# Two transfers cut smaller: the third x load in halves, and the last stores in finer pieces

## The chip, the cores and the metric

The kernel runs on one core of one Trainium2 chip. The metric is the device time of one execution in microseconds (us), as a median of repeated runs. All runs quoted here were with a granted TensorE clock of 0.95 to 1.00. A profile of one execution comes with each kernel. Its span (209.1 us before) is about 2 us shorter than the device time (211.0 us).

## The reference

```python
# x [16, 512, 1024], weight [1024, 768], bias [768], residual [16, 512, 768], all float32
return (np.matmul(x, weight) + bias + residual).astype(np.float32)
```

The kernel has to read 61.9 MB and write 25.2 MB. The matmul runs in bf16.

## The kernel before

There are 8192 rows: 64 tiles of 128 rows, in 8 super tiles of J = 8 tiles. A tile's x is cast to bf16 on ScalarE and transposed on TensorE. It then meets the weights in 8 steps of two matmuls each, 512 and 256 columns wide. GpSimd and VectorE add bias and residual into the residual's own buffer `ro`, and the result is stored from there. All large transfers are issued by one queue, that of SyncE (SP), in program order.

```python
J = 8; X_BUFS = 2; RO_BUFS = 4            # x: 2 super tiles in SBUF, residual/result: 4

def load_x(S, j0=0, j1=J):                # tiles j0..j1 of super tile S
    if S < n_s:
        if j0 == 0:
            x_sb[S] = ring(sb, "x_tile", S, X_BUFS, [P, J, K], FP32)
        K_(nc.sync.dma_start(out=x_sb[S][:, j0:j1, :], in_=x_d[S, :, j0:j1, :]))

def store(S, j0=0, j1=J, n0=0, nl=N):
    K_(nc.sync.dma_start(
        out=out_d[S, :, j0:j1, n0:n0 + nl], in_=ro[S][:, j0:j1, n0:n0 + nl]))
# ... (head: loads, weight casts, the first HEAD = 3 tiles)
for t in range(HEAD, n_t):
    cast(t + 2)
    S, j = divmod(t, J)
    if (t + 2) % J == J - 1:
        load_x(S + X_BUFS)
        load_res(S + X_BUFS)
        if 1 <= S < n_s - 1:
            store(S - 1)
    # ... (matmuls of tile t, transposes of t + 1, adds)
    if S == n_s - 1 and j == 0:
        store(S - 1)
    if S == n_s - 1 and j == J // 2:
        store(S, 0, J // 2)
    if S == n_s - 1 and j == J - 1:
        store(S, J // 2, j)               # tiles 4, 5 and 6 of the last super tile
t, S = n_t - 1, n_s - 1
for b, (n0, nl) in enumerate(chunks):     # last tile: 512 columns, then 256
    # ... (matmuls, add)
    store(S, J - 1, J, n0, nl)
```

## Time and profile before

| | before |
|---|---|
| device time, median of 6 runs | 211.01 us (210.88 to 211.19) |
| TensorE busy, share of the span | 96% |
| transfers of the SP queue, packet time as a share of 16 DMA engines' span | 97.8% |
| TensorE's one late wait for data | at 56 us, 0.8 to 0.9 us |
| last store: issued, landed | 204.9, 208.2 us |

These are lines of the page of the kernel before. "DMA" and "GB/s" cut the span into 40 slices. A digit is the busy share in tenths, as a mean over the core's 16 DMA engines. The `q` lines are DMA queues: packets, MB, and their packets' time as a share of 16 engines' span.

```profile
span 209.1 us, 3149 instructions
PE 201.1 (96%) x1274; PEld 130.8 (63%) x1299; DVE 105.0 (50%) x139; ACT 68.0 (33%) x68; POOL 115.6 (55%) x71
...
DMA  6999999999999999999999999999999999999966
GB/s 229 428 422 432 430 421 438 443 456 407 404 476 420 409 432 412 443 428 434 437 415 459 415 414 447 437 426 418 428 431 443 445 412 421 432 442 423 414 287 273
...
q1 hardware_dynamic: 5328, 87.03, 97.8%
q8 instruction: 10, 0.16, 0.3%
...
PE 70%; DMA 25%; issue 1%; ACT 1%; DVE 0%; POOL 0%; ACTq 0%; POOLq 0%
```

TensorE and the DMA engines are both full. The last line is the chain of waits that ended last. It is a quarter DMA, because it passes through loads of the head and of x. The longest piece of it is the third x load, of which these are the lines (start, duration, what):

```profile
22.74 33.22 DMA x_tile<-in_x_dram
...
56.05 1.05 ACT xb L87
...
57.15 0.66 PE pt L95 x4
```

The timeline of TensorE there (start, duration, engine, line, operation) shows how much this costs. L95 are a tile's transposes, 3.04 us apart in the steady state. Here one gap is 3.86 us.

```profile
53.29 0.60 PE L95 MATMUL pt<-ident,xb 128*128 128x128 f32 x4
...
57.15 0.66 PE L95 MATMUL pt<-ident,xb 128*128 128x128 f32 x4 [0.67 <-ACT xb L87]
...
60.25 0.60 PE L95 MATMUL pt<-ident,xb 128*128 128x128 f32 x4
```

At the end, these are the last three stores as SP issues them. The first is tiles 4 to 6; the `x2` are the two pieces of tile 7.

```profile
202.93 0.33 SPq L78 DMA_DIRECT2D out_dram<-ro  x1
...
204.39 1.55 SPq L78 DMA_DIRECT2D out_dram<-ro  x2
```

The table of stretches for the end follows (window, length, busy time and count of each engine, clock, DMA share, GB/s). The last two columns are what to read: the DMA share falls to 0.32 and recovers once the last stores are issued.

```profile
200.00:201.00 1.00, 1.00 (x9) 0.74 (x8) 0.43 (x1) 0.00 (x0) 0.00 (x0) 1.00 0.90 381
201.00:202.00 1.00, 1.00 (x8) 0.60 (x7) 0.32 (x2) 0.00 (x0) 0.00 (x0) 1.00 0.67 283
202.00:203.00 1.00, 1.00 (x7) 0.43 (x5) 0.90 (x1) 0.00 (x0) 0.00 (x0) 1.00 0.32 135
203.00:204.00 1.00, 1.00 (x9) 0.71 (x8) 0.33 (x1) 0.00 (x0) 0.00 (x0) 1.00 0.41 172
...
206.00:207.00 1.00, 0.00 (x0) 0.00 (x0) 0.00 (x0) 0.00 (x0) 0.00 (x0) 1.00 0.85 340
207.00:208.00 1.00, 0.00 (x0) 0.00 (x0) 0.00 (x0) 0.00 (x0) 0.00 (x0) 1.00 0.68 238
```

### The profile page before, as it was taken

What the parts mean: (1) busy time and instruction counts of PE and PEld (TensorE: products, weight loads), DVE (VectorE), ACT (ScalarE), POOL (GpSimd) and SP (SyncE); (2) the same over time, 40 slices, a digit from 0 to 9 for tenths busy, and PEclk for the clock granted to TensorE, in tenths of its full rate; (3) what the DMA queues carried; (4) which work ended last, traced back from release to release, by engine and by line L of the source; (5) the groups of instructions that cost most, each with busy time, mean ns of one, the idle gap of its engine ahead of it and who ended that gap; (6) DMA issues with size and microseconds to landing.
All of it is one profiled execution on the core that took longest, in us unless ns stands there. A gap on an engine that the chain in (4) does not pass through costs nothing.

```text
span 209.1 us, 3149 instructions
## 1 busy us (share of the span) xinstructions
PE 201.1 (96%) x1274; PEld 130.8 (63%) x1299; DVE 105.0 (50%) x139; ACT 68.0 (33%) x68; POOL 115.6 (55%) x71
## 2 busy tenths in 40 slices
PE   7999999999899999999999999999999999999991
PEld 2556666666566666666666666666666666666660
DVE  0646564455354455445545544554554455446551
ACT  2544315520283054323423252440543234322000
POOL 2000197819936655999499802994069900799000
PEclk9999999999999999999999999999999999999999
DMA  6999999999999999999999999999999999999966
GB/s 229 428 422 432 430 421 438 443 456 407 404 476 420 409 432 412 443 428 434 437 415 459 415 414 447 437 426 418 428 431 443 445 412 421 432 442 423 414 287 273
DMA packets 5344, 87.23 MB, mean 417 GB/s; under 512 B 593, under 2 KB 721, under 8 KB 1618
## 3 DMA queue, kind: packets, MB, share of 16 engines
q1 hardware_dynamic: 5328, 87.03, 97.8%
q8 instruction: 10, 0.16, 0.3%
q14 instruction: 4, 0.03, 0.0%
q10 hardware_dynamic: 2, 0.00, 0.0%
HBM read 61.87 MB, written 25.17 MB: 416 GB/s over the span
## 4 chain that ended last, share of the span: by engine, by line
PE 70%; DMA 25%; issue 1%; ACT 1%; DVE 0%; POOL 0%; ACTq 0%; POOLq 0%
PE po L104 60%; DMA x_tile<-in_x_dram 23%; PE pt L95 10%; DMA tmp<-in_bias_dram 2%; ACT xb L87 1%; DVE ro L131 0%; POOL ident masks.py:197 0%; ACTq L87 0%; POOL tmp L135 0%; POOLq L262 0%
## 5 line engine op out<-in xcount | busy, mean ns | idle before, releaser
L104 PE MATMUL po<-w_sb,xt 128*128 128x512 bf16 (+1 forms) x999 | 175.4, 324 | 1.4
L104 PEld LDWEIGHTS <-xt 128*128 128x128 bf16 x1024 | 100.1, 98 | 59.5 <-DVE xt L99 0.5
L87 ACT CAST xb<-x_tile 128x1024 bf16<-128x1024 f32 x62 | 63.2, 1045 | 115.5 <-PE pt L95 63.2
L121 POOL TENSOR_TENSOR ro<-ro,bias_sb 128x768 f32<-128x768 f32 x40 | 71.2, 1816 | 34.6 <-DMA ro<-in_residual_dram 24.6
L99 DVE COPY xt<-pt 128x512 f32<-128x512 f32 x64 | 44.2, 692 | 88.3 <-PE pt L95 88.2
L121 POOL TENSOR_TENSOR ro<-ro,tmp 128x768 f32<-128x768 f32 x24 | 43.1, 1816 | 42.3 <-DMA ro<-in_residual_dram 25.0
L131 DVE TENSOR_TENSOR ro<-po,ro 128x768 f32<-128x768 f32 (+2 forms) x41 | 38.0, 930 | 2.9 <-PE po L104 2.8
L95 PE MATMUL pt<-ident,xb 128*128 128x128 f32 x256 | 38.6, 274 | 0.7 <-ACT xb L87 0.7
L95 PEld LDWEIGHTS pt<-ident,xb 128*128 128x128 f32 x256 | 30.1, 142 | 9.2 <-ACT xb L87 1.3
L129 DVE TENSOR_TENSOR tmp<-po,bias_sb 128x768 f32<-128x768 f32 x24 | 22.8, 949 | 0.4 <-PE po L104 0.4
L170 PE MATMUL po<-warm 128*128 128x512 bf16 x15 | 6.1, 579 | 1.2 <-DVE warm L156 1.2
L176 ACT CAST w_sb<-ro 128x768 bf16<-128x768 f32 x4 | 3.3, 832 | 4.0 <-DMA ro<-in_weight_dram 4.0
L170 PEld LDWEIGHTS <-warm 128*128 128x128 bf16 x15 | 1.9, 132 | 4.1 <-issue 2.8
L87 DVE CAST xb<-x_tile 128x1024 bf16<-128x1024 f32 x2 | 1.4, 694 | 5.1 <-DMA x_tile<-in_x_dram 5.1
L178 DVE CAST w_sb<-ro 128x768 bf16<-128x768 f32 x4 | 2.2, 556 | 2.2 <-DMA ro<-in_weight_dram 2.2
L161 ACT ACT_TABLE_LOAD x1 | 1.3, 1283 | 2.0 <-POOL ident masks.py:199 2.0
L190 PE MATMUL po<-tmp 128*128 128x512 f32 (+1 forms) x4 | 1.5, 486 | 0.0
L198 DVE COPY bias_sb<-po 128x768 f32<-128x768 f32 x1 | 1.0, 958 | 0.1
L190 PEld LDWEIGHTS po<-tmp 128*128 128x128 f32 x4 | 0.7, 190 | 0.5 <-issue 0.5
L135 POOL MEMSET tmp<- 128x768 f32 x1 | 0.7, 737 | 0.3 <-POOLq L262 0.3
L156 DVE MEMSET warm<- 128x256 uint32 x1 | 0.3, 272 | 0.9 <-PEq L262 0.9
masks.py:199 POOL TENSOR_SCALAR_AFFINE_SELECT ident<-ident 128x128 f32<-128x128 f32 x1 | 0.3, 292 | 0.1
(8 smaller groups left out, 1.0 us busy)
## 6 DMA issues: line engine op xcount, KB each, us to landing
x_tile<-in_x_dram SPq DMA_DIRECT2D x6, 4096.0 KB, 29.4
ro<-in_residual_dram SPq DMA_DIRECT2D x7, 3072.0 KB, 18.0
out_dram<-ro SPq DMA_DIRECT2D x7, 3072.0 KB, 24.9
x_tile<-in_x_dram SPq DMA_DIRECT2D x2, 2048.0 KB, 23.9
x_tile<-in_x_dram SPq DMA_DIRECT2D x3, 1024.0 KB, 8.7
ro<-in_weight_dram SPq DMA_DIRECT2D x4, 768.0 KB, 9.1
ro<-in_residual_dram SPq DMA_DIRECT2D x2, 1536.0 KB, 20.9
out_dram<-ro SPq DMA_DIRECT2D x1, 1536.0 KB, 10.4
```

What stands on the lines that cost most here:

```text
L87: K_(copy(out=xb[t], in_=x_sb[t // J][:, t % J, :]))
L95: K_(nc.tensor.transpose(out=pt[:, c, :], in_=pairs[:, c * P:(c + 1) * P], identity=ident))
L99: K_(nc.vector.tensor_copy(out=xt[t], in_=pt))
L104: K_(nc.tensor.matmul(po[t][:, n0:n0 + nl], lhsT=both[:, e, :], rhs=w_sb[:, c, e, n0:n0 + nl], start=(i == 0), stop=(i == len(steps) - 1),))
L121: K_(nc.gpsimd.tensor_add(out=r, in0=r, in1=tmp[t] if t < EARLY else bias_sb))
L129: K_(nc.vector.tensor_add(out=tmp[t], in0=p, in1=bias_sb))
L131: K_(nc.vector.tensor_add(out=row(t, n0, nl), in0=p, in1=row(t, n0, nl)))
L161: K_(nc.scalar.copy(out=warm_a, in_=warm_a))
L170: K_(nc.tensor.matmul(warm_ps[:, 0:512], lhsT=warm[:, 0:P], rhs=warm, start=True, stop=True))
L176: K_(nc.scalar.copy(out=w_sb[:, c, e, :], in_=w_st[:, c, e, :]))
L178: K_(nc.vector.tensor_copy(out=w_sb[:, c, e, :], in_=w_st[:, c, e, :]))
L190: K_(nc.tensor.matmul(bias_ps[:, n0:n0 + nl], lhsT=ones, rhs=bias_row[:, n0:n0 + nl], start=True, stop=True,))
```

## The change

The intent is to remove the wait at 56 us, by making the first half of x available as soon as it has landed, and to shorten the end, by sending tiles 4 and 5 out without waiting for tile 6.

```diff
-            load_x(S + X_BUFS)
+            if S == 0:
+                load_x(X_BUFS, 0, J // 2)
+                load_x(X_BUFS, J // 2, J)
+            else:
+                load_x(S + X_BUFS)
             load_res(S + X_BUFS)
@@
+        if S == n_s - 1 and j == J - 2:
+            store(S, J // 2, j)
         if S == n_s - 1 and j == J - 1:
-            store(S, J // 2, j)
+            store(S, j - 1, j)
```

## The prediction

> **What bounds it now.** Two things at once. TensorE is busy 96% of the 209.1 us span (the page, part 1), at 3.04 us a tile (transposes start at 47.21, 50.25, 53.29 in the timeline). The DMA engines are as full: the per-slice line shows 9 from the second slice to the 38th, 430 GB/s between 100 and 180 us (stretch table). That is close to the 435 GB/s ceiling that the Trainium skill ("DMA: Bandwidth & Descriptors", Specifications) gives, so the 87.2 MB are a floor: the queue has no gap until about 201 us.
>
> **Where time is lost.**
> 1. Near 56 us. The chain of waits follows x of the third super tile from its issue at 22.74 to its landing at 55.95; its cast (1.05 us) and the transposes at 57.15 follow. Without the wait they would begin at 53.29 + 3.04 = 56.33; the next begin at 60.25 instead of 59.37. The stall is 0.8 to 0.9 us. TensorE waits for no data afterwards.
> 2. The tail. Tiles 4 to 6 (1152 KB) are issued at 202.93, the last two pieces at 204.39 and 204.94; the last lands near 208.2. But the DMA share is 0.90, 0.67, 0.32, 0.41 in the four microseconds from 200: some 1.7 us of DMA time is empty while tiles 4 and 5, finished at 199.86, wait for tile 6. Then 1.57 MB run at full rate from 203.75 to 207.8. This block of bytes sets the end, not the last matmul.
>
> **What the change does.**
> - x halves: the same bytes, one more issue of 0.33 us on a queue that runs ahead. 4.19 MB at 430 GB/s is 9.75 us, so the load really streams from about 46.2; the first half should land near 51.1, before it is needed. Tile 16's stall goes; the second half (near 56) is needed only by tile 20. Packets of 16 KB take 615 ns against 1213 for 32 KB: about 0.14 us more DMA time. TensorE runs 0.9 us earlier to its end.
> - Stores: tiles 4 and 5 (768 KB, 1.8 us at 430 GB/s) go out at about 199.0, while a backlog still flows; they fill the empty 1.7 us. Tile 6 follows at about 202.05, the last pieces at 203.5 and 204.1.
>
> **The sum.** The gains do not add. The queue is saturated, so a TensorE that is 0.9 us ahead cannot bring the earlier bytes out sooner; both parts reclaim the same empty 1.7 us. The store split alone should give about 1.4, the x split alone about 0.8, both about 1.5 (1.7 less 0.14 for packets). Check: the last issue at 204.1 plus about 2.4 (an estimate: 0.8 from issue to first packet as at 202.93, under a microsecond of queue and data, 0.4 to land) is 206.5, against 208.2. Span about 207.5; time 209.5 us, 0.7% faster. Range 208.9 to 210.2. Chances: faster by over 2% 0.01, within 2% 0.985, slower by over 2% 0.005.
>
> **What would show it.** TensorE's idle before the transposes near 57 us gone, tile 16's transposes near 56.3; last matmul near 203.6 instead of 204.5; first x half landing near 51; DMA share 0.9 or more until about 205; last store landing near 206.6.
>
> **What would make it wrong.** The last small stores taking over 2.5 us whatever the queue holds (gain nearer 0.9); the halves landing interleaved, so that the first comes no earlier (gain about 1.4); residual loads or reused buffers stalling a TensorE that is now ahead; a slower DMA rate at the end, with more writes in the mix.

## The result

| | before | after |
|---|---|---|
| device time, median of 6 runs | 211.01 us (210.88 to 211.19) | 210.84 us (210.74 to 211.01) |
| ratio of fast runs | | 0.9992 (95% interval 0.9979 to 1.0005) |

The times do not differ measurably, where 1.5 us had been predicted. A ratio in this document is the mean time of one kernel's fast runs over that of the other's in the same rounds, so it is not quite the ratio of the medians quoted.

The page after, in the lines that answer to those above:

```profile
span 209.0 us, 3151 instructions
PE 200.4 (96%) x1274; PEld 130.6 (63%) x1299; DVE 105.0 (50%) x139; ACT 67.6 (32%) x68; POOL 115.5 (55%) x71
...
DMA  6999999999999999999999999999999999999994
...
q1 hardware_dynamic: 5616, 87.03, 97.9%
q8 instruction: 10, 0.16, 0.3%
...
PE 96%; issue 1%; DVE 1%
```

The chain of waits no longer contains a DMA at all. It is tempting to read "PE 96%" as "TensorE is the bound"; experiment 6 shows that it is not. The timeline of TensorE after shows no stall (52.79 to 55.82 is 3.03 us):

```profile
52.79 0.60 PE L95 MATMUL pt<-ident,xb 128*128 128x128 f32 x4
...
55.82 0.60 PE L95 MATMUL pt<-ident,xb 128*128 128x128 f32 x4
...
58.86 0.60 PE L95 MATMUL pt<-ident,xb 128*128 128x128 f32 x4
```

SP's issues at the end, after: tiles 4 and 5, tile 6, and the two pieces of tile 7, the first of which goes out 1.4 us earlier than before:

```profile
198.50 0.33 SPq L78 DMA_DIRECT2D out_dram<-ro  x1
...
201.54 0.33 SPq L78 DMA_DIRECT2D out_dram<-ro  x1
...
203.00 0.87 SPq L78 DMA_DIRECT2D out_dram<-ro  x2
```

And the stretches at the end, after:

```profile
201.00:202.00 1.00, 1.00 (x6) 0.42 (x5) 0.51 (x1) 0.00 (x0) 0.00 (x0) 1.00 0.94 399
202.00:203.00 1.00, 1.00 (x9) 0.68 (x7) 0.69 (x1) 0.00 (x0) 0.00 (x0) 1.00 0.95 396
...
205.00:206.00 1.00, 0.00 (x0) 0.00 (x0) 0.00 (x0) 0.00 (x0) 0.00 (x0) 1.00 0.66 255
206.00:207.00 1.00, 0.00 (x0) 0.00 (x0) 0.00 (x0) 0.00 (x0) 0.00 (x0) 1.00 0.31 116
207.00:208.00 1.00, 0.00 (x0) 0.00 (x0) 0.00 (x0) 0.00 (x0) 0.00 (x0) 0.83 0.10 35
```

Everything local happened as intended. The stall is gone, TensorE's matmuls end at 203.06 instead of 204.45 us, and the hole in the DMA share at 201 to 204 us is filled. (0.5 us of that TensorE lead comes from the head, where this run began its first tile earlier. The kernels are equal there, and the head's timing moved by up to 0.5 us between profiles.) Yet the DMA share now fades slowly, 0.66, 0.31, 0.10, and the last store lands at the same time as before. A share of 0.10 need not be 16 engines at a tenth of their speed; it can be one or two engines still working, and the next table shows that it is.

The trace lets one see the single engines. According to the Trainium skill ("DMA: Bandwidth & Descriptors", Why a DMA increments its semaphore by 16 and not by 1), each engine that takes part in a transfer adds one to its semaphore when its own share has landed. The trace agrees: every large transfer leaves 16 separate increments. Sorted by time, they tell how far the engines have drifted apart. I worked this table out from these increments (us from the span's start):

```
                            issued   first engine   median   last engine   spread
before
  residual 0, tiles 0 to 3    6.86          23.89    24.05         25.36     1.47
  residual 7                160.73         175.83   177.08        178.73     2.89
  tiles 0-3, last super tile 193.91        201.21   202.78        204.30     3.09
  tiles 4-6                 202.93         206.92   207.02        207.12     0.21
  tile 7, 256 columns       204.92         207.95   208.04        208.18     0.22
after
  tiles 0-3, last super tile 192.52        201.20   202.77        204.44     3.25
  tiles 4-5                 198.50         203.02   204.60        206.27     3.25
  tile 6                    201.54         203.94   205.53        207.19     3.25
  tile 7, 256 columns       203.54         205.19   206.50        208.13     2.94
```

After the change, the fastest engine is done at 205.19, the median one at 206.50, and the slowest at 208.13. Before, the two slowest engines finished their backlog (their last packets of tiles 0 to 3) at 203.76 and 203.83, and the first packet of tiles 4 to 6 started at 203.75. So the hole in the mean DMA share belonged to the other engines. The slowest one had none, and it had the same bytes left to move in both kernels: it ended tiles 0 to 3 at 204.30 before and at 204.44 after. That the late block of stores was ready just as the slowest engine came free is a coincidence of this kernel.

### The profile page after: what moved, and what is told of

Same layout as the page of the kernel before. It is cut to its first block, busy times and chain, and to the rows that moved or that the text cites. A ratio compares the mean times of both kernels' runs of the same rounds, so it can differ in the third digit from the quotient of the medians.

```text
span 209.0 us, 3151 instructions
## 1 busy us (share of the span) xinstructions
PE 200.4 (96%) x1274; PEld 130.6 (63%) x1299; DVE 105.0 (50%) x139; ACT 67.6 (32%) x68; POOL 115.5 (55%) x71
## 3 DMA queue, kind: packets, MB, share of 16 engines
q1 hardware_dynamic: 5616, 87.03, 97.9%
## 4 chain that ended last, share of the span: by engine, by line
PE 96%; issue 1%; DVE 1%
PE po L104 79%; PE pt L95 13%; PE po L170 3%; PE po L190 1%; DVE xt L99 0%; DVE ro L131 0%; DVE warm L156 0%
## 5 line engine op out<-in xcount | busy, mean ns | idle before, releaser
L104 PE MATMUL po<-w_sb,xt 128*128 128x512 bf16 (+1 forms) x999 | 175.4, 324 | 1.4
L104 PEld LDWEIGHTS <-xt 128*128 128x128 bf16 x1024 | 100.1, 98 | 59.5 <-DVE xt L99 0.5
```

Source lines behind the costliest of these rows:

```text
L104: K_(nc.tensor.matmul(po[t][:, n0:n0 + nl], lhsT=both[:, e, :], rhs=w_sb[:, c, e, n0:n0 + nl], start=(i == 0), stop=(i == len(steps) - 1),))
```

## The experiments

**Theory A:** the slowest of the 16 DMA engines has no gap from the first load to the last store, and its last byte sets the time in both kernels. **Theory P** is my prediction: the mean share counts. **Theory C:** one part gains and the other loses. **Theory L:** the last small stores take some 4.6 us whatever lies ahead of them. Then, on why one engine is slowest: **F**, it carries instruction packets twice; **S**, it is slow by itself. Except for run 7, every ratio below is from five rounds.

### 1 and 2. Each part alone

Both are the kernel before with one hunk of the change. Experiment 1, x halves:

```diff
-            load_x(S + X_BUFS)
+            if S == 0:
+                load_x(X_BUFS, 0, J // 2)
+                load_x(X_BUFS, J // 2, J)
+            else:
+                load_x(S + X_BUFS)
```

Experiment 2, store split:

```diff
+        if S == n_s - 1 and j == J - 2:
+            store(S, J // 2, j)
         if S == n_s - 1 and j == J - 1:
-            store(S, J // 2, j)
+            store(S, j - 1, j)
```

> The x halves alone, with the old stores. Theory A (the slowest of the 16 DMA engines has no gap from start to end, and its last byte sets the time): TensorE's stall near 57 us goes and its last matmul comes near 203.3, the time stays at 211.0 us within 0.3. Theory P (as predicted, the mean share of the engines counts, and 1.7 us of DMA time were empty): 0.8 us faster, 210.2.

> The store split alone, with x of the third super tile in one piece. Theory A: 211.0 us within 0.3, the empty DMA share after 200 us moves to after 205 us. Theory P: 1.4 us faster, 209.6. Theory C (the two parts cancel: one gains, the other costs as much): this one or the x halves alone is at least 0.5 us faster than before, and the other slower.

| | time | ratio to before |
|---|---|---|
| 1, x halves alone | 211.11 us | 0.9993 (0.9980 to 1.0005) |
| 2, store split alone | 211.28 us | 0.9993 (0.9981 to 1.0006) |

The kernel before had a median of 211.51 us in these rounds, so only the ratios should be compared. Theory P is refuted: it wanted 0.996 and 0.993, outside both intervals. So is theory C, since neither part gains or loses. In both runs the last store again waits for a few late engines: the first engine lands at 206.99 and 206.83, thirteen of the 16 within 0.2 us of it, and the last at 208.77 and 208.74.

### 3 and 4. A shorter queue, with and without the change

786 kB of super tile 4 are not stored, in the changed kernel (3) and in the kernel before (4). Nothing waits for these bytes.

```diff
             if 1 <= S < n_s - 1:
-                store(S - 1)
+                store(S - 1, 2 if S == 5 else 0, J)
```

> The changed kernel, but tiles 0 and 1 of super tile 4 are not stored at all (wrong result on purpose): 786 kB less, 49 kB on each DMA engine, 1.83 us at 27 GB/s. Theory A: the end is set by the bytes of the slowest engine, so the time falls by 1.6 to 1.9 us against the changed kernel, to about 209.1. Theory L (the last small stores take some 4.6 us from issue to landing whatever lies ahead of them in the queue): no gain, 210.8.

> The kernel before, with the same 786 kB not stored (wrong result on purpose). Theory A: the backlog of the slowest engine ends near 202.0 instead of 203.8, but tiles 4 to 6 are still issued at 202.93 in one block of which the data starts at 203.75, so the end stays: 0 to 0.3 us faster, 210.7 to 211.0. That would make the change worth 1.5 us once the queue is 1.8 us shorter. If TensorE's end had nothing to do with it and bytes alone counted: 1.8 us faster, 209.2.

| | time | ratio to before |
|---|---|---|
| 3, the change, 786 kB less | 209.22 us | 0.9900 (0.9887 to 0.9913) |
| 4, before, 786 kB less | 211.19 us | 0.9993 (0.9981 to 1.0005) |

This separates the kernels. The changed one turns the missing bytes into time: 0.9992 less 0.9900 is 0.92% of 211, or 1.9 us (each against its own runs of before). The missing bytes are 49 kB per engine: eight packets of 18.4 kB, 0.69 us each in the trace, go in place of eight of 24.6 kB, 0.91 us each, which is 1.8 us less. The kernel before gains nothing, because it is then held up by its own late block of stores. The stretches show it. First those of experiment 3, then of experiment 4, where the queue lies all but empty from 200 to 204 us:

```profile
200.00:202.00 2.00, 2.00 (x12) 1.06 (x11) 1.29 (x2) 0.00 (x0) 0.00 (x0) 1.00 0.93 387
202.00:203.00 1.00, 1.00 (x8) 0.69 (x7) 0.27 (x1) 0.00 (x0) 0.00 (x0) 1.00 0.48 197
203.00:204.00 1.00, 0.50 (x5) 0.20 (x2) 0.85 (x2) 0.00 (x0) 0.00 (x0) 1.00 0.83 332
```

```profile
200.00:202.00 2.00, 2.00 (x15) 1.42 (x14) 0.74 (x2) 0.00 (x0) 0.00 (x0) 1.00 0.25 104
202.00:203.00 1.00, 1.00 (x7) 0.45 (x5) 0.86 (x1) 0.00 (x0) 0.00 (x0) 1.00 0.03 12
203.00:204.00 1.00, 1.00 (x8) 0.61 (x7) 0.23 (x2) 0.00 (x0) 0.00 (x0) 1.00 0.15 65
```

Theory L falls as well: in experiment 3 the last piece lands 3.1 us after its issue, not 4.6. So the kernel before stood at two limits at once. One is the slowest DMA engine's stream; the other is the last compute and the 1.57 MB issued behind it. The change lowers only the second.

### 5 and 6. Why one engine is slower, and whether TensorE bounds anything

The drift comes in steps. These are the 16 increments of each of five transfers in the kernel before, as lags behind the first of them, worked out from the trace (us; of the first transfer only the spread):

```
at  20.13: (x 0, tiles 6-7)  spread 0.49: no engine stands out
at  23.89: 0.00 0.02 0.04 0.05 0.11 0.12 0.13 0.14 0.18 0.22 0.24 0.25 0.29 0.41 0.43 | 1.47
at  44.67: 0.00 0.04 0.06 0.10 0.12 0.13 0.14 0.19 0.23 0.24 0.26 0.29 0.42 0.43 | 1.48 1.57
at 175.83: 0.00 0.00 0.06 0.29 0.54 0.67 0.95 1.13 1.38 1.50 1.57 1.58 1.65 1.69 1.83 | 2.89
at 197.59: 0.00 0.04 0.09 0.34 0.58 0.71 1.42 1.52 1.63 1.68 1.71 1.78 1.88 2.08 | 2.94 3.05
```

The packets of the page's line `q8 instruction`, 16384 bytes and about 1.07 us each, start at 21.98, 40.58, 61.18, 78.50, 99.27, 117.24, 135.44, 153.89, 174.91 and 193.34 us. The first leaves one engine a microsecond behind the next slowest, the second a second engine, and so on. The ninth and tenth hit engines that are behind already: at 168.53 us, before the ninth, the last engine was 1.84 us behind the first, and at 175.83 us 2.89.

The trace also shows what one such packet costs, and it is more than 1.07 us. The first takes from 21.98 to 23.05 us. The data packet that starts as it ends, at 23.04, takes 0.95 us, where others of its size take 0.46. All ten are followed by a data packet that is 0.36 to 0.55 us longer than its kind. Worked out from these numbers, each sets its engine back by 1.4 to 1.6 us.

The packets are 19 us apart on average, close to TensorE's own pace: 2573 recorded instructions in about 200 us are 256 in 19.9 us. (In experiment 5 below, with 2019 such instructions, there are eight packets, 24.1 us apart.) It fits the Trainium skill ("Runtime: NRT & Kernel Launch", Instruction fetch mechanics), by which instructions are fetched in 16 KiB blocks of 256 by a DMA queue that the sequencer drives itself.

Experiment 5 leaves out 280 of the 256-column matmuls, so that two packets go. Experiment 6 keeps these instructions and makes them narrow, 32 columns. The second piece of the edit below belongs to experiment 5 too: it marks these sums as ended, since their later steps are gone.

```diff
         for n0, nl in chunks:
+            if 16 <= t < 56 and n0 and i:      # experiment 5
+                continue
             mm(t, i, n0, nl)
 ...
-            start=(i == 0), stop=(i == len(steps) - 1),
+            start=(i == 0), stop=(i == len(steps) - 1) or (n0 > 0 and 16 <= t < 56),

-            mm(t, i, n0, nl)                   # experiment 6
+            mm(t, i, n0, 32 if 16 <= t < 56 and n0 and i else nl)
```

> The changed kernel with 280 of its 256-column matmuls left out (steps 1 to 7 of tiles 16 to 55, wrong result on purpose), so TensorE has some 560 instructions fewer and two to three of the ten 16 KB instruction packets of queue 8 go. Theory F (these packets, 1.07 us each on one DMA engine at a time, come round to the same engine twice and make it the slowest): the spread of landings at the end falls from 3.0 to about 1.8 us and the time falls by 1.0 to 1.5 us, to about 209.5. Theory S (some engine is slow by itself): spread and time as in the changed kernel, 210.8. TensorE has 30 us less work here, so see the next run for that.

> The changed kernel with the same 280 matmuls made 32 columns wide instead of left out (wrong result on purpose): as many instructions, as many instruction packets, but TensorE has at least 20 us less work. If TensorE's work bounds the time in any stage after the head: several us faster. Theory A with F: within 0.3 us of the changed kernel, 210.8, spread of the last landings still near 3 us.

| | time | ratio to before | instruction packets of q8 | TensorE busy | lag of the last engine at the last store |
|---|---|---|---|---|---|
| after | 210.84 us | 0.9992 | 10 | 200.4 us | 2.94 us |
| 6, narrow | 210.86 us | 0.9984 (0.9972 to 0.9997) | 10 | 186.7 us | 3.16 us |
| 5, left out | 209.84 us | 0.9933 (0.9920 to 0.9947) | 8 | 180.3 us | 2.54 us |

The lines of the pages behind it, first of experiment 6, then of experiment 5:

```profile
PE 186.7 (89%) x1274; PEld 114.3 (55%) x1299; DVE 105.3 (50%) x139; ACT 66.6 (32%) x68; POOL 115.6 (55%) x71
...
q8 instruction: 10, 0.16, 0.3%
```

```profile
PE 180.3 (87%) x1000; PEld 103.7 (50%) x1019; DVE 105.2 (51%) x139; ACT 66.5 (32%) x68; POOL 115.5 (55%) x71
...
q8 instruction: 8, 0.13, 0.3%
```

Taking 14 us of busy time from TensorE (I had expected 20) is worth nothing beyond noise: 0.9984 against 0.9992. TensorE's last matmul even ends at 200.01 us there, 3.0 us before that of the changed kernel, while the last store lands at 208.12 against 208.13. TensorE is not the bound, although the chain of waits says 96%. With the two packets gone as well, the time falls: 0.9933 over 0.9984 is 0.9949, which is 1.07 us, give or take 0.4 (an estimate from the two intervals).

That supports theory F, but does not settle it. I had expected a spread of 1.8 us, and 2.54 remained. What makes up the rest was not tested, and the traces hold two candidates besides theory S. The queue q14 has four instruction packets of 8 KB in every run. In the kernel before they take 0.31 to 0.33 us each and the data packets behind them are 0.32 to 0.66 us longer, so each sets an engine back as well, by 0.6 to 1.0 us. And in experiment 6 two data packets, at 136.87 and 137.19 us, take 2.2 and 2.3 us instead of 1.2, with no instruction packet beside them, so part of its 3.16 us has another cause.

### 7. Which engines lag

The tile `probe` is a new buffer of 8 partitions by 2 KB. Five small loads into it are put behind the store of tiles 0 to 3 of the last super tile.

```diff
             store(S, 0, J // 2)
+            for q in (8, 4, 2, 1, 8):
+                K_(nc.sync.dma_start(out=probe[0:q, :], in_=res2d[0:q, 0:512]))
```

> The changed kernel with five small loads (8, 4, 2, 1, 8 partitions of 2 KB) issued right behind the store of tiles 0 to 3 of the last super tile, after the last instruction packet. It asks which engines lag: by the Trainium skill (DMA: Bandwidth & Descriptors, Why a DMA increments its semaphore by 16 and not by 1) a transfer of k partitions, k up to 16, runs on the lowest-numbered k engines. If the lagging engines are among the low ones, the load of 8 partitions lands as late as that store's slowest engine (204.4 us); if the low half is the fast half, it lands near 201.5. Time 210.9, with at most 0.2 us added.

The time was 217.14 us, ratio 1.0282 (1.0263 to 1.0302), so the expected 0.2 us was badly wrong. All five loads write one buffer, so each waited for the one before, and SP's in-order queue held the last stores back behind them: tiles 4 and 5 were issued at 209.40 us instead of 198.50. From the wait list of the SP queue (total, times, longest, in us):

```profile
SPq L245 <- DMA probe<-in_residual_dram: 13.8, 4, 10.4
```

The first probe still answers a part. Its eight landings (201.66, 201.72, 202.04, 202.06, 203.25, 203.71, 204.26, 204.70) each follow one landing of the store ahead by 0.15 to 0.20 us, and among those are the store's two last, 204.06 and 204.50. So the two slowest engines are among the eight that a transfer of 8 partitions uses. By the Trainium skill ("DMA: Bandwidth & Descriptors", Why a DMA increments its semaphore by 16 and not by 1) these are the lowest-numbered eight; the trace shows eight landings, but not the engines' numbers. Four engines of these eight lag by less than 0.5 us, so they are not slow as a group. The probes of 4, 2 and 1 partitions were issued after the queue had drained and tell nothing; which two engines it is stays open.

### 8 and 9. Each part alone with the shorter queue

These are experiments 1 and 2, each with this one line more:

```diff
-                store(S - 1)
+                store(S - 1, 2 if S == 5 else 0, J)
```

They ask what each part is worth once the DMA limit is lower.

> The x halves alone, with 786 kB of super tile 4 not stored (wrong result on purpose). The DMA floor is 1.8 us lower here, so each part of the change should be worth what it does to the issues at the end. Tiles 4 to 6 go out near 202.0 in one block whose 0.8 us to the first packet and 1.57 MB then set the end: last landing near 207.1 against 208.2 of before, so 0.9 to 1.2 us faster than before: 209.9 to 210.2 where before is 211.1. If the slowest engine still set the end, as with both parts: 1.9 us.

> The store split alone, with the same 786 kB not stored (wrong result on purpose). Tiles 4 and 5 go out at 199.9 and use the freed time; the last piece is issued near 205.0 and needs at least the 1.7 us that the fastest engine needed in the runs before: last landing near 206.9, so 1.3 to 1.7 us faster than before: 209.4 to 209.8 where before is 211.1. If the last block of compute did not matter at all: 1.9 us, as with both parts.

| with 786 kB less | time | ratio to before | gain over experiment 4 |
|---|---|---|---|
| 4, neither part | 211.19 us | 0.9993 | |
| 8, x halves | 209.85 us | 0.9929 (0.9917 to 0.9941) | 0.64%, 1.35 us |
| 9, store split | 209.82 us | 0.9928 (0.9916 to 0.9940) | 0.65%, 1.37 us |
| 3, both | 209.22 us | 0.9900 | 0.93%, 1.96 us |

(The gains are differences of ratios, times 211 us; runs 8 and 9 were measured beside their own runs of before.) Both parts work, and they do not add: 1.35 and 1.37 alone, 1.96 together. In experiments 4, 8 and 9 all 16 engines end the last store within 0.24 us of each other, so there the late stores end the run; in experiment 3 they end 1.40 us apart, so the slowest engine does again. Against the kernel before, the store split gained 1.52 us, as expected, and the x halves 1.50 us, where 0.9 to 1.2 had been expected. TensorE's lead is larger here, which may be why: experiment 4 shows its first transposes after the x wait at 57.35 us, experiment 8 at 56.21.

No experiment pointed to a correct version faster than both kernels. The bytes are all needed, and experiment 5 gains only by leaving work out. In the kernel as it stands there is nothing to choose in time between before and after.

## Why the prediction was wrong

- **The stall near 57 us goes: right.** The transposes of tile 16 came 3.03 us after those ahead, and the first half of x landed at 51.20 us (predicted 51.1), the second at 56.08.
- **The store split fills the empty DMA share: right as a mean.** From 201 to 205 us the share is 0.94 to 0.98, as predicted.
- **"Some 1.7 us of DMA time is empty": this step failed.** I read a mean of 16 engines as if it were a queue that any byte could use. Every large transfer here leaves 16 increments, one of each engine, and a byte assigned to the slowest can't use another's gap. The slowest engine ended its backlog at 203.83 us and had new packets from 203.75: it had no empty time to reclaim. The 1.5 us thus became 0.17 us (medians), within noise.
- **The last store near 206.6: wrong, for the same reason.** The median engine did land at 206.50. The slowest landed at 208.13, and the completion waits for it.
- **"The 87.2 MB are a floor": right in kind, too low in size.** By the `q1` line each engine's data packets take 97.9% of 209.0 us, or 204.6 us. As the steps above suggest, the slowest engine was also held up by two instruction packets, 1.4 to 1.6 us each. The kernel before already stood at that limit.
- **"The gains do not add": right**, but it could only be seen with a shorter queue (experiments 3, 4, 8 and 9).
- I named four things that could make the prediction wrong, and none of them was the cause. Instruction packets, in plain sight in the page's third part, were not among them.

## What to carry to other kernels

When the DMA queues are full, ask for the slowest of the 16 engines, not the mean: compare the first and the last of a transfer's 16 completions, and when a mean share fades at the end (here 0.66, 0.31, 0.10 in three microseconds), look for one or two late engines. A kernel may stand at two limits at once; lowering one then shows correct local effects and no gain, and a run that lowers the other on purpose tells whether the change is worth keeping. A chain of waits that is all TensorE does not prove that TensorE is the bound; making its work shorter does.

## What the Trainium skill lacked or had wrong

- "Runtime: NRT & Kernel Launch" (Instruction fetch mechanics) calls the cost of crossing a 16 KiB block "mostly hidden". For TensorE it is: its matmuls of L104 waited 1.4 us in all. But each block here takes about 1.07 us of one DMA engine and sets it back by 1.4 to 1.6 us, and with full DMA queues the slowest engine sets the time: experiment 5 with 8 packets was 1.07 us faster than experiment 6 with 10, give or take 0.4.
- "DMA: Bandwidth & Descriptors" does not say how instruction packets are spread over the 16 engines. In the kernel before, the steps in the landings suggest that the first eight fell on eight different engines and the next two on engines that were behind already; by the end the engines were 3.1 to 4.0 us apart in the runs with ten packets.
- "DMA: Bandwidth & Descriptors" (Queues, rings and completion order) puts instruction refill in row 14. In this trace the ten packets at TensorE's pace are in q8, and q14 has only four of 8 KB during the span. Whether the profile's queue numbers are that page's rows, no run here shows.
- "DMA: Bandwidth & Descriptors" (Where 436 GB/s comes from) says that about 358 GB/s of HBM bind a transfer between HBM and SBUF, a sentence that lacks its condition. The page's section Measured gives that rate for the case that both cores that share an HBM domain stream at once. Here, with one core in use, loads and stores together ran at 430 GB/s from 100 to 180 us.
